# Four row buffers with y built in place, and the chunk stage's loads in written order, in a hybrid decoder step on Trainium2

## The chip, the cores and the metric

The kernel runs on one core of a Trainium2 chip. Its engines are PE (TensorE, matmuls, with PEld for the weight loads), DVE (VectorE), ACT (ScalarE), POOL (GpSimd) and SP (SyncE), which here does nothing but issue DMA transfers. Each engine works through its own list of instructions in order, and semaphores order them against each other. The metric is device microseconds of one execution, and a kernel's time is the median of several runs.

## The reference, cut to what matters

One layer of a decoder with two branches, for 1024 prompt positions and 64 sample positions (8 samples of 8 positions each). Pooling branch `P` and state-space branch `S` share one input projection, and are merged by gates.

```python
proj = h @ w_in
u_pool, z_pool, z_ssm, xbc, dt_raw, g_raw = jnp.split(proj, SPLITS, axis=-1)
p, pool_new = pool_mix(u_pool, pool_buf, pos0, pool_w, pool_scale)
p = (p * jax.nn.silu(z_pool)) @ w_pool_out
xbc_c, conv_new = causal_conv(xbc, conv_buf, conv_w, conv_b)
...
y, ssm_new = ssd(xs, dt, A, Bm, Cm, ssm_state)
y = (y + d_skip.astype(jnp.float32)[:, None] * xs).reshape(b, L, D_INNER)
y = rmsnorm(y * jax.nn.silu(z_ssm.astype(jnp.float32)), ssm_norm_g)
s = y.astype(x.dtype) @ w_ssm_out
gates = jax.nn.sigmoid(g_raw)
m = gates[..., :D_MODEL] * p + gates[..., D_MODEL:] * s
x = x + gate[:, None] * (m @ w_o)
```

`ssd` goes over the prompt in 8 chunks of 128 positions, for 4 groups of 8 heads, and carries a state from chunk to chunk:

```python
def step(h, inp):
    xq, dq, Bq, Cq = inp
    acs = jnp.cumsum(dq * Ag, axis=1)
    seg = acs[:, :, None] - acs[:, None, :]
    decay = jnp.exp(jnp.where(mask, seg, -jnp.inf))
    cb = jnp.einsum('bign,bjgn->bijg', Cq, Bq)
    att = cb[..., None] * decay * dq[:, None]
    y = jnp.einsum('bijge,bjgep->bigep', att, xq)
    y = y + jnp.einsum('bign,bige,bgepn->bigep', Cq, jnp.exp(acs), h)
    ...
```

## The kernel before, in words

The kernel goes in stages: the norm and the first gate products; the input projection (seven products in place of eight for each pair of column blocks) with the convolutions and the pooling beside it; the samples' state-space part beside the last of these; then the chunk stage; then a tail with the last group's output products, w_o and the final norm. Intermediate results lie in DRAM (`xbc_d`, `z_d`, `gp_d`, `ys_d` and others). A planner decides the order of the instructions on each engine from a simulated timeline, unless the text fixes it: `in_line(engines)` chains all instructions of the named engines that were written since the last call, so that they run in written order, and `behind(engine)` puts what is written under it behind that engine's latest instruction.

The chunk stage is the one that the change touches. It does two things side by side.

- 32 rows, one for each group g and chunk c: the generator `chunk(g, c)`, in steps divided by `yield`. Step 1 loads the row's x, B and C (`xb`, six blocks of 128 x 128, line 1491) and the decay exponents (`dec`, 512 KB, line 1187). Step 2 makes the exponentials: `cE` on ACT (1498), the mask `far` on POOL (1192), eight exponentials on ACT (1201). Step 3 loads silu(z) (`sz`, 1504), transposes x and B on PE (1507, 1509), and scales on DVE (1518, 1520, 1525, 1527). Step 4 does the row's products on PE (1532, 1213, 1216) and the state (1538, 1540), adds D times x into a tile `v` on DVE (1545), and calls `finish`. `finish` multiplies `v` by `sz` on DVE (1468), rounds it into the high half `yh` on ACT (1470), squares it on ACT (1471), subtracts for the low half `yl` on POOL (1472), and sums the squares on POOL (1473 to 1479). A fifth step, in the last chunk of a group alone, stores the state.
- 32 products of weights with a whole block of rows, from the generator `pieces`: 8 of the pooling branch (`P_unit`, which loads a gate row `sg` at 1718, multiplies it at 1721 and stores it), then 8 for each of the groups 0 to 2 (`S_unit`). Each is three PSUM blocks of 12 matmuls (359 to 361). The weights come from DRAM by `ready` (459 and 460) into tiles with four buffers. `products(t)` has made 2.56 blocks for each row by time t, beyond the first four.

From row 13 on, `wo_splits` adds the splitting of w_o into high and low halves, 16 pieces: load (1771), high half on ACT (1775) and its store, low half on POOL (1777) and its store by SP (1781). It has two buffers for the raw pieces, so a load waits for the store of the low half two pieces before.

`sample_end(g)` brings in the 64 sample positions of a group: it loads their silu(z) (1483) and their sums `ys` (1485) and calls `finish`, once in eight rows.

In turn i of the main loop (line 1802) come: a step of `wo_splits`, step 3 of row i+1, products up to i+0.4, a fifth step of row i-1 if there is one, a step of `wo_splits`, step 4 of row i, step 1 of row i+3, step 2 of row i+2, products up to i+1. PE runs in written order throughout, DVE and ACT only in the part before the loop, SP in the planner's order.

Buffers before: `xb` three, `dec` three, `cE` two, `sz` three, `v` two (shared by rows and samples), PSUM tiles `mm` three.

Of the kernel before, what the change touches and what calls it, by code (L numbers as in the profile page):

```python
# [11 lines left out]
ALU = mybir.AluOpType  # L12
# [8 lines left out]
P = 128  # L21
# [4 lines left out]
NS = 64  # L26
# [7 lines left out]
NC = SEQ // CH  # L34
# [12 lines left out]
def tile_pool_ssd_step(  # L47
# [9 lines left out]
    def nm(s):  # L57
        uid[0] += 1
        return f"{s}_{uid[0]}"
# [37 lines left out]
    def PB():  # L97
        return psB.tile([P, 512], F32, tag="ps", name=nm("ps"))
# [8 lines left out]
    def const(shape, name, dt=F32):  # L107
        return cp.tile(shape, dt, tag=name, name=name)
# [5 lines left out]
    V = nc.vector  # L114
# [224 lines left out]
    def in_line(engines, begin=False):  # L339
        traced = nc.cur_bb.bb.instructions  # L340
        for i in traced[len(traced) if begin else line[0]:]:
            if i.engine in engines:
                if i.engine in line[1]:
                    tc.add_manual_dep(i, line[1][i.engine], mybir.DependencyInfo(
                        mybir.DependencyClass.NoSync, mybir.DependencyReason.DATA), reason="in_line")
                line[1][i.engine] = i.name
        line[0] = len(traced)
# [20 lines left out]
    Dv = const([P, 16], "Dv")  # L368
# [815 lines left out]
    def decays(dec, g, c):  # L1184

        S = P if c < NC else NS
        load(dec, acs_d[c, 8 * g:8 * g + 8, :S].partition_broadcast(S))
# [275 lines left out]
    def ckt(shape, tag, bufs=2):  # L1463
        return (cl if tag in CKL else ca if tag in ("dec", "xb", "cE") else ck).tile(list(shape), F32, tag=tag, name=nm(tag), bufs=bufs)

    def finish(g, o, S, v, sz):

        V.tensor_tensor(v, v, sz, ALU.mult)
        yhc = yh[g][:, :, o:o + S]
        act(yhc, v, AF.Copy)  # L1470
        act(sz, v, AF.Square)
        nc.gpsimd.tensor_tensor(yl[g][:, :, o:o + S], v, yhc.bitcast(F32), ALU.subtract)
        nc.gpsimd.tensor_tensor(sz[:, 0:2], sz[:, 0:2], sz[:, 2:4], ALU.add)
        sa = sq_acc[:, o:o + S]
        if g == 0:
            nc.gpsimd.tensor_tensor(sa, sz[:, 0], sz[:, 1], ALU.add)
        else:
            nc.gpsimd.tensor_tensor(sz[:, 0], sz[:, 0], sz[:, 1], ALU.add)
            nc.gpsimd.tensor_tensor(sa, sa, sz[:, 0], ALU.add)

    def sample_end(g):
        sz = ckt([P, 4, P], "sz", 3)[:, :, :NS]
        load(sz, z_d[g][:, :, SEQ:])
        v = ckt([P, 4, P], "v")[:, :, :NS]
        load(v, ys_d[g])
        finish(g, SEQ, NS, v, sz)

    def chunk(g, c):
        o = c * P
        xb = ckt([P, 6, P], "xb", 3)  # L1490
        load(xb, xbc_d[g][:, :, o:o + P])
        Bf, Cf = xb[:, 4], xb[:, 5]
        dec = ckt([P, 8, P], "dec", 3)
        decays(dec, g, c)
        yield
        if c > 0:
            cE = ckt([P, 8, P], "cE")
            act(cE, dec, AF.Exp, scale=-1.0)
        if g > 0 or c > 0:
            far(dec, c)  # L1500
            exps(dec, g, c)
            yield
        sz = ckt([P, 4, P], "sz", 3)
        load(sz, z_d[g][:, :, o:o + P])
        px = PB()
        for q in range(4):
            nc.tensor.transpose(px[:, q * P:(q + 1) * P], xb[:, q], ident)
        pbc = PB()
        nc.tensor.transpose(pbc[:, :P], Bf, ident)
        mm(pbc[:, P:2 * P], Bf, Cf, start=True, stop=True)  # L1510
        bt = ckt([P, P], "bt", 2)
        act(bt, pbc[:, :P], AF.Copy)
        if c > 0:
            act(pbc[:, 2 * P:3 * P], Cf, AF.Copy)
        pxv = px.rearrange("p (h d) -> p h d", d=64)
        heads = slice(8 * g, 8 * g + 8)
        xd = ckt([P, 8, 64], "xd", 2)
        V.tensor_tensor(xd, pxv, dtT[:, c, heads].unsqueeze(2).to_broadcast([P, 8, 64]), ALU.mult)
        xw = ckt([P, 8, 64], "xw", 1)
        V.tensor_tensor(xw, pxv, wdT[:, c, heads].unsqueeze(2).to_broadcast([P, 8, 64]), ALU.mult)  # L1520
        if g == c == 0:
            yield
            far(dec, c)
            exps(dec, g, c)
        V.tensor_tensor(dec, dec, pbc[:, P:2 * P].unsqueeze(1).to_broadcast([P, 8, P]), ALU.mult)
        if c > 0:
            V.tensor_tensor(cE, cE, pbc[:, 2 * P:3 * P].unsqueeze(1).to_broadcast([P, 8, P]), ALU.mult)
        yield
        if c == 0:
            yh[g], yl[g] = [Y4(hs if g % 2 else hp) for _ in range(2)]  # L1530
        pu = PC()
        mm(pu, bt, xw.rearrange("p h d -> p (h d)"), start=True, stop=True)  # L1532
        pi = inner(xd, dec, P, *((hst[g], cE) if c > 0 else ()))
        hn = ckt([P, 512], "hst", 2)
        if c == 0:
            act(hn, pu, AF.Copy)
        else:
            nc.gpsimd.tensor_tensor(hn.rearrange("p (h d) -> p h d", d=64), hst[g].rearrange("p (h d) -> p h d", d=64),
                                    Elb[:, c, heads].unsqueeze(2).to_broadcast([P, 8, 64]), ALU.mult)
            V.tensor_tensor(hn, hn, pu, ALU.add)  # L1540
        hst[g] = hn

        v = ckt([P, 4, P], "v")
        for q in range(4):
            V.scalar_tensor_tensor(v[:, q], xb[:, q], Dv[:, 4 * g + q:4 * g + q + 1], pi[:, q], ALU.mult, ALU.add)
        finish(g, o, P, v, sz)
        if c == NC - 1:
            yield
            pt = PB()
            for q in range(4):  # L1550
                nc.tensor.transpose(pt[:, q * P:(q + 1) * P], hn[:, q * P:(q + 1) * P], ident)
            fo = ckt([P, 4, P], "fo", 1)
            act(fo, pt.rearrange("p (q n) -> p q n", n=P), AF.Copy)
            store_(new_ssm_p[0, 0, 8 * g:8 * g + 8].rearrange("(q h) p n -> (h p) q n", h=2), fo)
# [192 lines left out]
    prods = []  # L1747
# [7 lines left out]
    def pieces():  # L1755
        ws = first_ws
        nxt = len(ws)
        for i, (pf, run) in enumerate(prods):
            while nxt < len(prods) and nxt <= i + 1:
                ws[nxt] = prods[nxt][0]()  # L1760
                nxt += 1
            yield from run(ws.pop(i))
# [3 lines left out]
    def wo_splits():  # L1766
        raws = {}
        for n in range(18):
            if n < 16:
                raws[n] = ck.tile([P, 512], F32, tag="pw", name=nm("pw"), bufs=2)  # L1770
                load(raws[n], w_o[0, n // 2 * P:n // 2 * P + P, n % 2 * 512:n % 2 * 512 + 512])
            yield
            if 0 < n < 17:
                hi = ck.tile([P, 512], F32R, tag="ph", name=nm("ph"), bufs=1)
                act(hi, raws[n - 1], AF.Copy)
                store_(wo_d[(n - 1) // 2][:, 0, (n - 1) % 2 * 512:(n - 1) % 2 * 512 + 512], hi.bitcast(F32))
                nc.gpsimd.tensor_tensor(raws[n - 1].bitcast(F32R), raws[n - 1], hi.bitcast(F32), ALU.subtract)
                lo = raws.pop(n - 1)
            yield
            if 0 < n < 17:  # L1780
                load(wo_d[(n - 1) // 2][:, 1, (n - 1) % 2 * 512:(n - 1) % 2 * 512 + 512], lo)
    wos = wo_splits()
    RATE = 2.56
    FRONT = 4
# [5 lines left out]
            next(pc_, None)  # L1790
            made += 1

    first_engines = (mybir.EngineType.PE, mybir.EngineType.Activation, mybir.EngineType.DVE)
    in_line(first_engines, True)
    next(seq[0])
    for _ in range(FRONT - 1):
# [5 lines left out]
    for i in range(len(seq)):  # L1802
        if i > 12:
            with behind(mybir.EngineType.Activation), behind(mybir.EngineType.SP), behind(mybir.EngineType.Pool):
                next(wos, None)
        if i + 1 < len(seq):
            next(seq[i + 1])
        products(i + 0.4)
        if i > 0:
            next(seq[i - 1], None)  # L1810
        if i > 12:
            with behind(mybir.EngineType.Activation), behind(mybir.EngineType.SP), behind(mybir.EngineType.Pool):
                next(wos, None)
        next(seq[i], None)
        if i % NC == 3:
            sample_end(i // NC)
        if i + 3 < len(seq):
            next(seq[i + 3])
        if i + 2 < len(seq):
            next(seq[i + 2])  # L1820
        products(i + 1.0)
    next(seq[-1], None)
    for it in (pc_, wos):
        for _ in it:
            pass
    in_line((mybir.EngineType.PE,))
    right.__exit__(None, None, None)
    while right_all:
        right_all.pop().__exit__(None, None, None)
# [152 lines left out]
    for i in range(8):  # L1982
# [7 lines left out]
        if last_:  # L1990
            q, s3 = hs.tile([P, T], F32, tag="sq", name="q", bufs=1)[:, :D], const([P, 4], "s3")
# [61 lines left out]
```

## Time and profile before

| | us |
|---|---|
| median of 3 runs | 1296.55 |
| lowest, highest | 1295.5, 1297.77 |
| the profiled execution | 1301.79 |
| its span, from the first instruction to the last | 1300.1 |
| mean granted clock of PE in it | 0.992 |

The profile is of one execution on the chip. In its lists, a line such as `L1507` is a line of the kernel, `out<-in` names the tiles by the program's names, and `x4` counts instructions that were merged. `PE` is the matmul, `PEld` the weight load, `SPq` a DMA issue on SP. In a row in order of time the first number is the start, the second the duration, and the bracket at its end gives the idle time of the engine just before it and what ended it. A row of waits gives the total, how often, and the longest. Two parts of the page show where the span goes in 40 equal slices and over the chain of work that ended last:

```profile
PE   7999999999999999999999999989999999999998
...
DMA  9837345465455544444565566988768788574621
...
PE 62%; issue 7%; DMA 6%; POOL 4%; DVE 3%; ACT 2%; ACTq 0%; SPq 0%; POOLq 0%; DVEq 0%
```

A digit is the busy share of a slice of 32.5 us in tenths. The chunk stage is about slices 26 to 35, in which the 16 DMA engines are busier than in most of the rest.

### The profile page before, as it was taken

The page shows a single profiled execution, that of the slowest core. Times are in us where ns is not written, and L with a number is a line of the kernel's source. Part 1 is how long each engine was busy: PE and PEld are TensorE (multiplying, and loading weights), DVE is VectorE, ACT ScalarE, POOL GpSimd, SP SyncE. Part 2 cuts the span into 40 slices and gives each one's busy share as a digit, 9 for nine tenths or more (in the row PEclk, how much of TensorE's full clock was granted, in tenths as well). Part 3 has the DMA queues.
Part 4 walks back from the last instruction along what each step waited for, and adds up shares of the span by engine and source line. Part 5 has one row for each costly group of instructions (what it writes and reads, how often), then busy time and mean ns, then how long its engine had stood idle before and what let it go on. Part 6 is the DMA issues. An engine that isn't in the chain of part 4 may idle for free.

```text
span 1300.1 us, 26323 instructions
## 1 busy us (share of the span) xinstructions
PE 1263.0 (97%) x9739; PEld 1173.4 (90%) x9739; DVE 901.5 (69%) x1608; ACT 662.4 (51%) x1528; POOL 668.3 (51%) x563
## 2 busy tenths in 40 slices
PE   7999999999999999999999999989999999999998
PEld 6779999989999999999999999978898888999786
DVE  4685778966979688776776765667676777476433
ACT  4665347364656655556556544555676655201111
POOL 1007669676869777565444435245566758214000
PEclk9999999999999999999999999999999999999999
DMA  9837345465455544444565566988768788574621
GB/s 330 253 108 226 115 148 175 145 207 162 139 170 198 174 154 135 155 144 134 169 193 173 174 183 200 343 263 264 248 212 281 243 286 262 177 260 160 227 104 51
DMA packets 233793, 251.68 MB, mean 194 GB/s; under 512 B 31265, under 2 KB 177905, under 8 KB 233658
## 3 DMA queue, kind: packets, MB, share of 16 engines
q1 hardware_dynamic: 161568, 171.60, 42.1%
q10 hardware_dynamic: 72098, 78.41, 17.8%
q8 instruction: 77, 1.26, 0.4%
q14 instruction: 50, 0.41, 0.1%
HBM read 167.06 MB, written 83.01 MB: 192 GB/s over the span
## 4 chain that ended last, share of the span: by engine, by line
PE 62%; issue 7%; DMA 6%; POOL 4%; DVE 3%; ACT 2%; ACTq 0%; SPq 0%; POOLq 0%; DVEq 0%
PE ps L608 6%; PE ps L609 6%; PE ps L610 6%; PE mm L608 6%; PE mm L610 6%; PE mm L609 5%; PE mm L359 4%; PE mm L360 3%; PE mm L361 3%; PE ps L1213 2%; PE ps L1999 2%; PE ps L2001 2%; PE ps L2000 2%; PE pc L1532 2%; POOL wlo L168 2%
## 5 line engine op out<-in xcount | busy, mean ns | idle before, releaser
L168 POOL TENSOR_TENSOR wlo<-rawA,whi 128x512 fp32r<-128x512 f32 x120 | 179.9, 1503 | 176.3 <-ACT whi L165 101.5
L168 POOL TENSOR_TENSOR wlo<-raw,whi 128x512 fp32r<-128x512 f32 x92 | 149.1, 1627 | 122.8 <-ACT whi L165 111.9
L359 PE MATMUL mm<-Y,whi 128*128 128x352 f32 (+1 forms) x480 | 165.7, 345 | 0.6 <-DVE G L1902 0.5
L360 PE MATMUL mm<-Y,whi 128*128 128x352 f32 (+1 forms) x480 | 159.4, 332 | 0.3 <-DVE Y L1569 0.3
L361 PE MATMUL mm<-Y,wlo 128*128 128x352 f32 (+1 forms) x480 | 158.7, 331 | 0.0
L608 PE MATMUL mm<-Y,whi 128*128 128x272 f32 x496 | 146.6, 296 | 0.7 <-DVE GA L624 0.5
L608 PE MATMUL ps<-Y,whi 128*128 128x272 f32 x496 | 144.2, 291 | 2.7 <-ACT o L808 2.1
L610 PE MATMUL mm<-Y,wlo 128*128 128x272 f32 x496 | 144.5, 292 | 2.2 <-POOL wlo L168 1.5
L609 PE MATMUL ps<-Y,whi 128*128 128x272 f32 x496 | 143.8, 290 | 0.0
L610 PE MATMUL ps<-Y,wlo 128*128 128x272 f32 x496 | 143.4, 289 | 0.0
L609 PE MATMUL mm<-Y,whi 128*128 128x272 f32 x496 | 142.9, 288 | 0.0
L1056 DVE SCALAR_TENSOR_TENSOR GA<-GA,cvT,GA 128x1112 f32<-128x1112 f32 x72 | 129.6, 1803 | 0.8 <-ACT GA L1053 0.7
L165 ACT ACTIVATE whi<-rawA 128x512 fp32r<-128x512 f32 x125 | 78.3, 627 | 91.4 <-PE ps L609 47.3
L165 ACT ACTIVATE whi<-raw 128x512 fp32r<-128x512 f32 x96 | 58.9, 627 | 105.2 <-DVE raw L554 48.0
L359 PEld LDWEIGHTS mm<-Y,whi 128*128 128x128 f32 x480 | 91.9, 191 | 7.1 <-issue 4.8
L610 PEld LDWEIGHTS mm<-Y,wlo 128*128 128x128 f32 x496 | 93.6, 189 | 4.0 <-POOL wlo L168 2.4
L608 PEld LDWEIGHTS ps<-Y,whi 128*128 128x128 f32 x496 | 94.0, 190 | 3.3 <-ACT o L808 2.3
L608 PEld LDWEIGHTS mm<-Y,whi 128*128 128x128 f32 x496 | 93.4, 188 | 3.3 <-ACT whi L165 0.7
L1201 ACT ACTIVATE dec<-dec,acT 128x128 f32<-128x128 f32 (+1 forms) x288 | 86.5, 383 | 18.4 <-POOL dec L1192 18.0
L609 PEld LDWEIGHTS mm<-Y,whi 128*128 128x128 f32 x496 | 93.7, 189 | 0.9
L609 PEld LDWEIGHTS ps<-Y,whi 128*128 128x128 f32 x496 | 94.1, 190 | 0.0
L610 PEld LDWEIGHTS ps<-Y,wlo 128*128 128x128 f32 x496 | 94.1, 190 | 0.0
(448 smaller groups left out, 3764.3 us busy)
## 6 DMA issues: line engine op xcount, KB each, us to landing
rawA<-in_w_in SPq DMA_DIRECT2D x46, 512.0 KB
dec<-acs_d SPq DMA_DIRECT2D x32, 512.0 KB
xbc<-GA ACTq DMA_DIRECT2D x24, 512.0 KB
xb<-xbc SPq DMA_DIRECT2D x32, 384.0 KB
rawA<-in_w_in SPq DMA_DIRECT2D x32, 256.0 KB
pw<-in_w_ssm_out ACTq DMA_DIRECT2D x32, 256.0 KB
ws<-ph ACTq DMA_DIRECT2D x32, 256.0 KB
ws<-pw SPq DMA_DIRECT2D x32, 256.0 KB
```

The lines of the kernel that those rows point to most:

```text
L165: ins = act(hi[:, :, :ncols], raw[:, :, :ncols], AF.Copy)
L168: (eng or nc.gpsimd).tensor_tensor(lo[:, :, :ncols], raw[:, :, :ncols], hi[:, :, :ncols].bitcast(F32), ALU.subtract)
L359: mm(ps[:, :n], a, rh[k][:, o:o + n], start=(k == 0), stop=False)
L360: mm(ps[:, :n], a, rl[k][:, o:o + n], start=False, stop=False)
L361: mm(ps[:, :n], b, rh[k][:, o:o + n], start=False, stop=(k == nk - 1))
L608: mm(p, hi, ah, start=(k == 0), stop=False)
L609: mm(p, hi, al, start=False, stop=False)
L610: mm(p, lo, ah, start=False, stop=(k == 3))
L1056: V.scalar_tensor_tensor(d[:, :n], rp[:, k:k + n], cvT[:, 24 * k + mc:24 * k + mc + 1], d[:, :n], ALU.mult, ALU.add)
L1201: act(dec[:, h], dec[:, h], AF.Exp, bias=acT[:S, c, 8 * g + h:8 * g + h + 1], scale=-1.0)
L1213: mm(o[hh], xd[:S, 2 * q + hh, :], dec[:S, 2 * q + hh], start=True, stop=state is None)
L1532: mm(pu, bt, xw.rearrange("p h d -> p (h d)"), start=True, stop=True)
```

## The change

Five edits, all in the chunk stage:

- `v` is no tile of its own for a row but the first four blocks of the row's `xb`; the multiply-add 1545 works in place, and so does `finish`. `xb` has four buffers. The samples' `v` is a tile of its own with one buffer, now contiguous.
- `sample_end` becomes a generator: it loads at the row with i % 8 = 2 and finishes at the row with i % 8 = 4; before, both were at i % 8 = 3.
- `pieces` asks for weights up to two products ahead, not one.
- `wo_splits` loads a raw piece and splits the piece before it in one step, and stores the low half in the next; before, the load came with the store of the low half before it, and the split in the step between.
- SP joins the engines whose instructions are chained in written order, in the part before the loop and in the loop.

```diff
     def sample_end(g):
         sz = ckt([P, 4, P], "sz", 3)[:, :, :NS]
         load(sz, z_d[g][:, :, SEQ:])
-        v = ckt([P, 4, P], "v")[:, :, :NS]
+        v = ckt([P, 4, NS], "v", 1)
         load(v, ys_d[g])
+        yield
         finish(g, SEQ, NS, v, sz)
 
     def chunk(g, c):
         o = c * P
-        xb = ckt([P, 6, P], "xb", 3)
+        xb = ckt([P, 6, P], "xb", 4)
...
-        v = ckt([P, 4, P], "v")
+        v = xb[:, 0:4]
         for q in range(4):
-            V.scalar_tensor_tensor(v[:, q], xb[:, q], Dv[:, 4 * g + q:4 * g + q + 1], pi[:, q], ALU.mult, ALU.add)
+            V.scalar_tensor_tensor(v[:, q], v[:, q], Dv[:, 4 * g + q:4 * g + q + 1], pi[:, q], ALU.mult, ALU.add)
         finish(g, o, P, v, sz)
...
-            while nxt < len(prods) and nxt <= i + 1:
+            while nxt < len(prods) and nxt <= i + 2:
                 ws[nxt] = prods[nxt][0]()
...
                 raws[n] = ck.tile([P, 512], F32, tag="pw", name=nm("pw"), bufs=2)
                 load(raws[n], w_o[0, n // 2 * P:n // 2 * P + P, n % 2 * 512:n % 2 * 512 + 512])
-            yield
             if 0 < n < 17:
                 hi = ck.tile([P, 512], F32R, tag="ph", name=nm("ph"), bufs=1)
...
             yield
             if 0 < n < 17:
                 load(wo_d[(n - 1) // 2][:, 1, (n - 1) % 2 * 512:(n - 1) % 2 * 512 + 512], lo)
+            yield
...
-    first_engines = (mybir.EngineType.PE, mybir.EngineType.Activation, mybir.EngineType.DVE)
+    first_engines = (mybir.EngineType.PE, mybir.EngineType.Activation, mybir.EngineType.DVE, mybir.EngineType.SP)
...
-        if i % NC == 3:
-            sample_end(i // NC)
+        if i % NC == 2:
+            ends = sample_end(i // NC)
+            next(ends)
+        if i % NC == 4:
+            next(ends, None)
...
-    in_line((mybir.EngineType.PE,))
+    in_line((mybir.EngineType.PE, mybir.EngineType.SP))
```

## The prediction

> **What bounds the kernel now.** I read the page first, then the busy times by stretch, the waits, the engines' rows in order of time, and SP's own waits.
>
> ```profile
> span 1300.1 us, 26323 instructions
> PE 1263.0 (97%) x9739; PEld 1173.4 (90%) x9739; DVE 901.5 (69%) x1608; ACT 662.4 (51%) x1528; POOL 668.3 (51%) x563
> ```
>
> PE is busy for 97% of the span, and the change touches only the chunk stage, about 817 to 1140 us. So the question is how much PE time that stage loses. The columns below are PE, PEld, DVE, ACT and POOL busy, then the granted clock, the DMA share and GB/s.
>
> ```profile
> core 0: us, PE busy (x) PEld busy (x) DVE busy (x) ACT busy (x) POOL busy (x), PEclk, DMA share, GB/s
> 817.00:866.00 49.00, 48.40 (x358) 43.42 (x357) 36.49 (x61) 28.91 (x75) 18.68 (x20) 1.00 0.93 308
> 866.00:881.00 15.00, 10.96 (x68) 8.74 (x66) 7.63 (x14) 5.80 (x16) 5.62 (x8) 0.77 0.82 264
> 881.00:1024.00 143.00, 143.00 (x1164) 127.36 (x1164) 102.32 (x176) 89.80 (x233) 88.80 (x105) 1.00 0.79 251
> 1024.00:1049.00 25.00, 22.16 (x172) 19.50 (x171) 19.55 (x36) 16.89 (x46) 14.89 (x17) 1.00 0.87 271
> 1049.00:1094.00 45.00, 44.89 (x355) 39.72 (x354) 31.74 (x55) 27.28 (x67) 33.06 (x38) 1.00 0.87 266
> 1094.00:1108.00 14.00, 12.12 (x90) 10.17 (x90) 12.03 (x24) 8.64 (x25) 9.77 (x14) 0.88 0.80 244
> ...
> 876.50:880.50 4.00, 4.00 (x15) 3.85 (x15) 3.36 (x9) 3.35 (x11) 1.69 (x2) 0.55 0.90 282
> ...
> 1102.50:1106.50 4.00, 4.00 (x16) 3.81 (x16) 3.94 (x9) 2.03 (x7) 2.25 (x3) 0.64 0.87 272
> ```
>
> The loss sits in three places: 4.04 us idle from 866 to 881, 2.84 from 1024 to 1049, 1.88 from 1094 to 1108. Behind the first and the last the clock is down: 0.55 of four microseconds (1.80 us lost) and 0.64 of four (1.44 us). Elsewhere PE is full, 143.00 of 143. What PE waited for, from its rows in order of time:
>
> ```profile
> 873.18 1.02 PE L1507 MATMUL ps<-ident,xb 128*128 128x128 f32 x4 [2.24 <-DMA xb<-xbc]
> 876.00 0.45 PE L1509 MATMUL ps<-ident,xb 128*128 128x128 f32 x1 [1.81 <-DVE cE L1527]
> ...
> 1036.69 0.55 PE L1507 MATMUL ps<-ident,xb 128*128 128x128 f32 x3 [1.33 <-DMA xb<-xbc]
> ...
> 1047.64 0.63 PE L1507 MATMUL ps<-ident,xb 128*128 128x128 f32 x4 [1.08 <-DMA xb<-xbc]
> ...
> 1101.65 0.80 PE L1507 MATMUL ps<-ident,xb 128*128 128x128 f32 x4 [1.88 <-DMA xb<-xbc]
> ```
>
> Four of the five are the transposes of a row (L1507) waiting for its `xb` to land, 6.53 us. The fifth, 1.81, is a PSUM buffer that DVE freed late. DVE was late for a reason of its own, in its waits and rows:
>
> ```profile
> DVE v L1468 <- DMA v<-ys: 17.2, 4, 7.4
> ...
> 872.05 0.43 DVE L1468 TENSOR_TENSOR v<-v,sz 128x256 f32<-128x256 f32 x1 [7.42 <-DMA v<-ys]
> ...
> 1089.89 0.83 DVE L1468 TENSOR_TENSOR v<-v,sz 128x256 f32<-128x256 f32 x1 [3.50 <-DMA v<-ys]
> ```
>
> Four times, once a group, DVE stands before the samples' sums `ys`, which are loaded and used in the same turn. The two waits quoted precede the first and the last loss; the other two, 6.3 us together, precede none.
>
> **The change, part by part.**
>
> *Row buffer and y in place.* The four multiply-adds L1545 and everything in `finish` keep engine, shape and count, so no work is added or removed; only `v` lies in the row's own `xb`. Three `xb` buffers become four. Today the load for row r+3 waits for row r's L1545; the chain of waits shows it:
>
> ```profile
> 1034.25 1.25 POOL Y L1472
> ...
> 1039.57 1.11 DVE v L1545 x4
> 1040.68 0.03 DVE G L1742
> 1040.71 6.79 DMA xb<-xbc
> ...
> 1095.71 5.80 DMA xb<-xbc
> ```
>
> L1545 ends at 1040.68, the load goes at 1040.71, lands 6.79 us later, and PE had waited 1.08 us. After the change that load waits for the previous row's last reader, POOL's subtraction L1472, which ended at 1035.50: 5.2 us earlier, against the 1.08 needed. The largest of the four waits is 2.24. So all four, 6.53 us, should go where POOL is as prompt as here.
>
> *Samples' sums two rows ahead.* The loads move from the turn in which they are used to two turns before it. The pace of a row:
>
> ```profile
> L1532 PE MATMUL pc<-xw,bt x64: 590/592/596, 831.2 to 1115.4; 128*128 128x512 f32 x64
> ...
> SPq L1771 <- DMA wo<-pw: 50.5, 14, 5.4
> SPq L459 <- PE mm L361: 35.0, 13, 9.0
> SPq L1504 <- POOL sq_acc L1479: 19.0, 12, 2.6
> SPq L1718 <- DMA m<-R: 18.9, 5, 6.3
> ```
>
> 31 row steps from 831.2 to 1115.4 are 9.2 us each, so the sums get some 18 us; the longest wait is 7.42. DVE's 17.2 us go, and with them PE's 1.81. One `v` buffer of its own suffices: it is used once in eight rows. The `sz` rotation is as before, one extra allocation in eight.
>
> *Clock.* If the gaps go, the 1.80 and 1.44 us go too: 3.24. The Trainium skill's page "TensorE: Matmul & The Clock Gate", section "HAM oscillation — how this bites in real kernels", has it that idle gaps above about 3.4 us drop the clock. By that rule the 1.88 us gap would cost nothing further and the sum would be smaller by 1.44; the 0.64 behind that gap says otherwise, so the row decides.
>
> *SP in written order.* The last rows above are SP's own waits. The longest, 50.5 us, is the raw w_o load (L1771) waiting for the store of the low half whose buffer it takes; the moved `yield` puts half a row between the two, so this falls mostly away. What a wait blocks is everything written behind it. Per row that is: w_o load, `sz` of the next row, weights and gate rows, low-half store, `xb` and `dec` three rows on. The pace is set by `dec`, which waits for row r's products, so SP comes by once a row; each `xb`, `sz` and weight load has more than one row of lead, 9.2 us, against 5.8 to 6.8 to land. I cost this at nothing; it hides behind the products on PE. The ends for the range: no gain, and the 16.2 us of the slower rival.
>
> *Weights two products ahead.* Today's order already issues them as soon as one of the four buffers is free (35.0 us of waits for L361 are these), thus three or more products ahead. Written order makes that two. A product is three PSUM blocks, and 2.56 blocks go with a row, so 10.8 us each: 21 us of lead. Nothing gained, nothing lost.
>
> *Gate rows of the pooling products.* These, L1718, are the one load that comes later. Products 1 to 7 now load their `R` in the order in which the product starts; today they run ahead (and wait, 18.9 us, for older stores).
>
> ```profile
> 819.18 0.42 SPq L1718 DMA_DIRECT2D R<-gp  x1
> ...
> 827.28 0.55 DVE L1721 TENSOR_TENSOR R<-mm,R 128x384 f32<-128x384 f32 x1
> ...
> 1025.06 0.17 PE mm L359
> ```
>
> From issue to use 8.1 us lie here, an upper bound of what the load needs. A product's first block is 12 matmuls at 0.17 us, 2.0 us, so DVE may stand up to 6.1 us at L1721, seven times. The bounds: DVE waits of some 3.1 us (the two without loss) cost PE nothing, so the lower end is 0; 3.50 and 7.42 us came with gaps of 1.88 and 4.04, so at 6.1 perhaps 3, seven times 21 us. The wait is nearer the lower end, since `mm` has three PSUM buffers and the block that needs the same one starts 10.8 us later: I take 2.0.
>
> **Sum.** 6.53 + 1.81 + 3.24 = 11.58 gained, 2.0 given back: 9.6 us. The profiled execution goes from a span of 1300.1 (1301.79 with what lies around it) to 1290.5. The runs shown have a median of 1296.55, 5.2 below that execution; less 9.6 this is **1287.0**. Its own range: down to 1282.2, if the remaining idle time goes too (0.42 in the three places, 0.60 and 0.11 in their neighbours) and the clock loss of 866 to 881 is the whole 0.23 × 15 = 3.45 instead of 1.80; up to 1291 with 6 us given back instead of 2.0.
>
> **Rivals.**
>
> *Gate rows late.* Three or four of the seven DVE waits cost PE about 2 us each: 7.5 given back, 1292.5. For it: 0.93 DMA share from 817 to 866, where most of these loads fall. Against it: DVE is idle for 12.5 of those 49 us.
>
> *It does not do what it says.* The row's load is freed earlier but leaves no earlier, since the written order puts it behind `sz` (19.0 us of waits for POOL) and the low-half store; the gaps stay or move: 1296.5. For it: right after a samples' turn the `sz` buffer asked for was released only one row ago. Against it: a late `sz` in front of `xb` is one wait of some ten microseconds in eight rows.
>
> *Slower: the row's reload now hangs on POOL.* L1472 must end the landing time before the transposes four rows on. In one stretch of today's run it doesn't; POOL stands behind a mask that waits for ACT:
>
> ```profile
> POOL dec L1192 <- ACT cE L1498: 29.3, 6, 14.3
> ...
> 1048.81 1.30 POOL L1472 TENSOR_TENSOR Y<-v,Y 128x512 fp32r<-128x512 f32 x1 [1.83 <-ACT Y L1470]
> ...
> 1071.88 2.56 POOL L1472 TENSOR_TENSOR Y<-v,Y 128x512 fp32r<-128x512 f32 x2 [1.47 <-ACT Y L1470]
> ...
> 1054.97 0.60 PE L1507 MATMUL ps<-ident,xb 128*128 128x128 f32 x4
> ...
> 1074.36 0.60 PE L1507 MATMUL ps<-ident,xb 128*128 128x128 f32 x4
> ```
>
> By count these are rows 22 and 24 (ends 1050.11 and about 1073.16) and the transposes of 26 and 28, 4.86 and 1.20 us later. With 5.8 to 6.8 to land, PE would stand 0.9 to 1.9 and 4.6 to 5.6 us, plus about 1.6 of clock: 8.1 at the middle for a group. In one group the change still wins 3.5; from two groups on it loses, 16.2 − 11.6 = 4.6, and with the 2.0 above 6.6: 1303. Against it: the low-half store and the mask's `dec` load, which made POOL late there, stood behind the 50.5 us. The Trainium skill's page "DMA: Bandwidth & Descriptors", section "Anatomy of one DMA", says that a DMA's semaphore wait is spent on the issuing sequencer before dispatch; SP's rows agree, and this is why a late POOL would hold the weights and `dec` as well, and why I don't go lower with this case.
>
> **How the numbers follow.** Forecast 0.55, gate rows late 0.15, no effect 0.12, slower 0.18. 0.2% (2.6 us) is about what a measurement of this kernel tells from none; the three runs lie within 2.3 us. Faster is the first two, 0.70; same 0.12; slower 0.18. The range 1282 to 1299 holds the first three, and leaves out most of the fourth.
>
> **What would show it.** Right: no PE wait for `xb` above 0.5 us and none of DVE for `ys`; granted clock 1.00 from 866 to 881 and 1094 to 1108; SP's wait L1771 far under 50.5. The 2.0 would be DVE's wait at L1721 for the gate rows, absent today. Wrong: PE waits for `xb` whose load left right after L1472 (the slower case); DVE waits for gate rows with PE gaps before 900 us (the first rival); or gaps of the same size at other rows.

## The result, and the profile after

| | before | changed |
|---|---|---|
| median, us | 1298.66 | 1305.33 |
| lowest, highest, us | 1295.5, 1308.41 | 1299.13, 1310.13 |
| the profiled execution, us | 1301.79 | 1308.79 |
| its mean granted clock | 0.992 | 0.99 |

Both medians are of 18 runs. The ratio is 1.0047, with a 95% interval of 1.003 to 1.0064: the change makes the kernel slower by about 6 us, where 1287.0 was forecast in a range that ends at 1299. Line numbers of the changed kernel are one higher than before's from the loads of `chunk` on, up to the w_o load (the lines behind it, 1775 to 1781, are as before): the transposes are L1508 and L1510, the loads of `xb` and `sz` L1492 and L1505, the multiply-add L1546, the gate row's load and multiply L1719 and L1722, the w_o load L1772.

The page of the changed kernel:

```profile
span 1307.1 us, 26274 instructions
PE 1263.8 (97%) x9739; PEld 1174.2 (90%) x9739; DVE 899.7 (69%) x1608; ACT 662.5 (51%) x1528; POOL 669.5 (51%) x563
...
PE 58%; issue 8%; DMA 8%; POOL 6%; DVE 4%; ACT 2%; SPq 0%; ACTq 0%; POOLq 0%; DVEq 0%
```

Busy times are those of before within 2 us. The work is the same. Of the 7.0 us between the spans of the two profiled executions PE's busy time takes 0.8; in the other 6.2 PE stood. In the chain that ended last, DMA has gone from 6% to 8% and POOL from 4% to 6%.

The busy times by stretch, with the columns as before (PE, PEld, DVE, ACT, POOL, clock, DMA share, GB/s):

```profile
864.00:880.00 16.00, 11.20 (x70) 9.35 (x69) 9.87 (x19) 4.98 (x13) 5.51 (x7) 0.79 0.82 271
...
1018.00:1024.00 6.00, 3.16 (x28) 2.70 (x25) 4.01 (x8) 0.95 (x3) 3.75 (x5) 1.00 0.83 236
1024.00:1057.00 33.00, 33.00 (x266) 29.17 (x266) 22.48 (x39) 20.48 (x52) 20.33 (x22) 1.00 0.91 305
1057.00:1080.00 23.00, 20.17 (x158) 17.76 (x157) 17.74 (x29) 12.58 (x33) 15.37 (x19) 1.00 0.60 199
1080.00:1092.00 12.00, 9.40 (x67) 8.21 (x66) 7.58 (x18) 6.24 (x16) 7.06 (x9) 0.86 0.90 295
1092.00:1110.00 18.00, 18.00 (x149) 16.04 (x148) 15.44 (x25) 11.95 (x29) 14.83 (x18) 1.00 0.92 296
```

The loss sits in four places now: 4.80 us idle from 864 to 880, 2.84 from 1018 to 1024, 2.83 from 1057 to 1080, 2.60 from 1080 to 1092; behind the first and the last the clock is down. The last of the three losses of before is gone: from 1092 to 1110 PE is busy for 18.00 of 18 us, at a clock of 1.00. What PE waited for, from its rows in order of time:

```profile
870.34 0.69 PE L359 MATMUL mm<-Y,whi 128*128 128x384 f32 x1 [4.80 <-DVE R L1722]
...
1023.86 0.63 PE L1508 MATMUL ps<-ident,xb 128*128 128x128 f32 x4 [2.84 <-DMA xb<-xbc]
...
1059.79 0.66 PE L1508 MATMUL ps<-ident,xb 128*128 128x128 f32 x4 [1.56 <-ACT fo L1554]
...
1061.72 0.33 PE L1510 MATMUL ps<-ident,xb 128*128 128x128 f32 x1 [1.27 <-DVE cE L1528]
...
1083.42 0.63 PE L1508 MATMUL ps<-ident,xb 128*128 128x128 f32 x4 [2.60 <-DMA xb<-xbc]
```

So a gate row, the `xb` of row 22, a PSUM buffer before row 26, and the `xb` of row 28 (rows are counted from 0, eight to a group). PE's 9739 matmuls stand in the same order in both traces, so the start of each after can be set against the start of the same one before. This sum over single rows, worked out beside the profile's views, gives the account. The left column is the time of before.

| stretch of before, us | later at its begin, at its end, us | so | what lies there |
|---|---|---|---|
| 0 to 817 | 0, 1.37 | +1.4 | the stages ahead, untouched |
| 817 to 868 | 1.37, 9.29 | +7.9 | new: the gate row, its clock |
| 868 to 884 | 9.29, 2.63 | −6.7 | gone: the gaps of 2.24 and 1.81, their clock |
| 884 to 1015 | 2.63, 3.54 | +0.9 | |
| 1015 to 1020 | 3.54, 6.56 | +3.0 | new: `xb` of row 22 |
| 1020 to 1050 | 6.56, 3.11 | −3.5 | gone: the gaps of 1.33 and 1.08 |
| 1050 to 1058 | 3.11, 6.30 | +3.2 | new: PSUM before row 26 |
| 1058 to 1080 | 6.30, 10.64 | +4.3 | new: `xb` of row 28, its clock |
| 1080 to 1110 | 10.64, 6.70 | −3.9 | gone: the gap of 1.88, its clock |
| 1110 to the end | 6.70, 7.01 | +0.3 | |

The five gaps of before are gone, and 14.1 us came from that. New ones took 18.4, and 2.6 are spread. Why the new ones arose stands in the waits. First DVE's for the gate rows, from 800 to 1150 us:

```profile
DVE R L1722 <- DMA R<-gp: 13.9, 6, 4.2
```

Then SP's own in the same stretch:

```profile
SPq L1781 <- POOL pw L1777: 38.8, 9, 6.0
SPq L1492 <- ACT sz L1471: 28.2, 8, 5.2
SPq L1492 <- POOL Y L1472: 21.4, 11, 12.9
...
SPq L1772 <- DMA wo<-pw: 17.3, 10, 4.3
SPq L1505 <- POOL sq_acc L1479: 13.6, 7, 8.1
SPq L1505 <- ACT sz L1471: 11.1, 3, 5.7
```

DVE's wait for `ys` has gone from 17.2 to 0.9, and SP's wait for the store of the low half has gone from 50.5 to 17.3. But now SP stands for the low half's subtraction (38.8), for the readers of the row buffer (28.2 and 21.4) and for free `sz` buffers (13.6 and 11.1), each time at the head of its list. SP's issues in order of time show what stood behind it, in three places: before the gate row, before row 22's `xb`, and before row 28's.

```profile
860.81 0.52 SPq L1505 DMA_DIRECT2D sz<-z  x1
...
862.51 0.43 SPq L1719 DMA_DIRECT2D R<-gp  x1
...
1016.27 0.52 SPq L1505 DMA_DIRECT2D sz<-z  x1
...
1017.56 0.52 SPq L1492 DMA_DIRECT2D xb<-xbc  x1
...
1066.21 0.39 SPq L1781 DMA_DIRECT2D wo<-pw  x1
1079.61 0.53 SPq L1492 DMA_DIRECT2D xb<-xbc  x1
```

An `sz` load keeps SP from 853.0, the end of the issue before it, to 860.81, and three issues on, at 862.51, goes the gate row, 4.5 us after PE had ended the block that it is for (858.0 by PE's rows). It lands at 869.7, when DVE has stood for it 3.71 us and PE for DVE's PSUM buffer nearly 4.80. An `sz` load after the samples' turn keeps it from 1006.2 to 1016.27, and at 1017.56 goes row 22's `xb`, 6.3 us before PE takes it: 3.5 us before PE was free for it, and 2.84 in which PE stood. The load of row 28's `xb` itself keeps it from 1066.6 to 1079.61. What that one waited for stands in the chain of waits:

```profile
1078.30 1.30 POOL Y L1472
1079.61 3.67 DMA xb<-xbc
```

This is row 24's subtraction. It ends at 1079.60, the load leaves at 1079.61, lands 3.67 us later, and PE stands. DVE had finished row 24's product with `sz` at 1065.6: from there to POOL's end it is 14.0 us.

The fourth place, before row 26, has a longer chain. SP had stood from 1037.6 to 1043.60 for the low half of a w_o piece, and row 25's `dec` left behind that store:

```profile
1043.60 0.32 SPq L1781 DMA_DIRECT2D wo<-pw  x1
...
1044.64 0.64 SPq L1187 DMA_DIRECT2D dec<-acs_d  x1
```

ACT waited 4.14 us for it, until 1050.85, and was late from there on with the copies that row 26's PSUM buffers hang on. That the rest of the delay follows from this wait is read from the order of ACT's rows and was not tested.

### The profile page after: what moved, and what is told of

Its sections match the earlier page's. It is cut to its first block, busy times and chain, and to the rows that moved or that the text cites. A ratio compares the mean times of both kernels' runs of the same rounds, so it can differ in the third digit from the quotient of the medians.

```text
span 1307.1 us, 26274 instructions
## 1 busy us (share of the span) xinstructions
PE 1263.8 (97%) x9739; PEld 1174.2 (90%) x9739; DVE 899.7 (69%) x1608; ACT 662.5 (51%) x1528; POOL 669.5 (51%) x563
## 4 chain that ended last, share of the span: by engine, by line
PE 58%; issue 8%; DMA 8%; POOL 6%; DVE 4%; ACT 2%; SPq 0%; ACTq 0%; POOLq 0%; DVEq 0%
PE ps L608 6%; PE ps L609 6%; PE ps L610 6%; PE mm L608 6%; PE mm L610 6%; PE mm L609 5%; PE mm L359 3%; PE mm L360 3%; PE mm L361 3%; PE ps L2004 2%; PE ps L2003 2%; PE ps L2005 2%; PE ps L1213 2%; POOL G L1912 2%; DMA dec<-acs_d 1%
```

## The experiments

Three theories stood for the new gaps. **Written order**: SP's list is now in written order, so a wait for an `sz` buffer or a gate row asked for too late holds up what is due sooner. **In place**: the row buffer hangs on POOL, as the prediction's slower rival had it. **By chance**: the gaps are accidents of one execution. Each experiment ran in five rounds beside the kernel before; the ratios are to that, with 95% intervals. "PE waits" names the waits of PE above 1 us from 810 to 1150 us in the profiled execution.

### e1_planner: the change without the written order

```diff
-    first_engines = (mybir.EngineType.PE, mybir.EngineType.Activation, mybir.EngineType.DVE, mybir.EngineType.SP)
+    first_engines = (mybir.EngineType.PE, mybir.EngineType.Activation, mybir.EngineType.DVE)
...
-    in_line((mybir.EngineType.PE, mybir.EngineType.SP))
+    in_line((mybir.EngineType.PE,))
```

> The changed kernel with SP back in the planner's order; the four buffers, y in place, the samples' sums and the w_o steps stay. If the written order of SP is the whole loss (one late load holds all behind it), the forecast's gain of about 11 us comes out: some 1287 where before is 1298.7. If y in place is the loss, since the row's buffer hangs on the low half's subtraction, the planner's order moves the other loads past it but the late row stays: about 1300, and PE still waits near 1080 us for xb. Gate rows go early again, so no PE gap before 900 us in either case.

1293.68 us against 1298.01, 0.9966 (0.9957 to 0.9976). PE waits: 2.21 before row 26 and 3.53 for row 28's `xb`, no others. The gate row and row 22 cost nothing here; the places of rows 26 and 28 stay. So the first two gaps come from the written order; the last two arise without it as well. The two ratios, 1.0047 and 0.9966, though not from the same rounds, are about 10.5 us apart, close to the 7.9 and 3.0 that the account gives to the first two places.

### e2_own_sz: the samples' silu(z) in a tile of its own

```diff
-        sz = ckt([P, 4, P], "sz", 3)[:, :, :NS]
+        sz = ckt([P, 4, NS], "zs", 1)
```

> The changed kernel with a tile of their own for the samples' silu(z), so that the rows' three sz buffers rotate undisturbed. If the sz load after a samples' turn is what holds SP (7.7 us before 1016.3 in the changed kernel's trace, then xb at 1017.6 for a transpose due at 1020.7), the gap of 3.0 us there goes, and the gate row behind the sz at 860.8 comes 7 us earlier, so the gap of 5 us at 865 shrinks too: 6 to 10 us less than the changed kernel. If SP is held by something else, no difference.

1297.69 against 1298.01, 0.9998 (0.9985 to 1.0011). The gap before row 22 is gone, and its `xb` leaves 9.4 us before PE is free for the transposes, not 3.5. The gate row's gap has become one of 2.75 for a later product's. 4.43 before row 26 and 1.03 for row 28 stay. That one runs through `dec`, as rows of this experiment show, from POOL, SP, ACT and DVE in turn:

```profile
1042.27 1.28 POOL L1472 TENSOR_TENSOR Y<-xb,Y 128x512 fp32r<-128x512 f32 x1
...
1043.58 0.53 SPq L1492 DMA_DIRECT2D xb<-xbc  x1
1044.20 0.58 SPq L1187 DMA_DIRECT2D dec<-acs_d  x1
...
1049.70 1.06 ACT L1499 ACTIVATE cE<-dec 128x1024 f32<-128x1024 f32 x1 [2.84 <-DMA dec<-acs_d]
...
1050.95 0.28 ACT L1515 ACTIVATE ps<-xb 128x128 f32<-128x128 f32 x1
...
1052.46 1.22 DVE L1528 TENSOR_TENSOR cE<-cE,ps 128x1024 f32<-128x1024 f32 x1
...
1053.93 1.09 PE L1508 MATMUL ps<-ident,xb 128*128 128x128 f32 x4 [4.43 <-DVE cE L1528]
```

Row 22's subtraction ends at 1043.55 and frees the buffer for row 26's `xb`, which leaves at once and lands in time. But row 26's `dec` is written behind it on SP. It lands when ACT has waited 2.84 us for it; row 25's copy is behind that on ACT, DVE's multiply behind the copy, and the PSUM buffer of row 26's transposes behind the multiply.

### e3_gate_ahead: gate rows asked for one product ahead

```diff
-            if m == 0:
-                sg = first_g[0]
-            else:
-                sg = R()
-                with behind(mybir.EngineType.SP):
-                    load(sg, gp_d[m])
+            sg = first_g[m]
+            if m < 7:
+                first_g.append(R())
+                load(first_g[m + 1], gp_d[m + 1])
```

> The changed kernel with each gate row loaded one product earlier. If DVE's wait for the gate row makes the gap at 865 us (5.0 us and the low clock behind it), that gap goes and 6 to 8 us with it, about back to the kernel before; DVE's waits for gate rows (13.9 us) go to under 3. If the gap comes from the sz wait in front of it alone, the row is still held at that place and the gap stays.

1296.03 against 1298.01, 0.9986 (0.9975 to 0.9997). The gate row's gap is gone and nothing comes in its place there. PE waits: 3.26 for row 22's `xb`, 2.85 for row 28's.

### e4_first_row_v: a `v` of its own for a group's first row

```diff
-        v = xb[:, 0:4]
+        v = ckt([P, 4, P], "vr", 1) if c == 0 else xb[:, 0:4]
...
-            V.scalar_tensor_tensor(v[:, q], v[:, q], Dv[:, 4 * g + q:4 * g + q + 1], pi[:, q], ALU.mult, ALU.add)
+            V.scalar_tensor_tensor(v[:, q], xb[:, q], Dv[:, 4 * g + q:4 * g + q + 1], pi[:, q], ALU.mult, ALU.add)
```

> The changed kernel, but the first row of each group builds y in a tile of its own (one buffer more), as all rows did before. Theory: the first row of the last group can't write its high half until PE has ended the products of the group two before, whose Y tile it takes, and in place this holds the row's xb and SP for 12.9 us, until 1079.6. Then the gap of 2.8 us at 1080 us and the low clock behind it go: 4 to 5 us less than the changed kernel. Rival, POOL being late in general (mask behind ACT): other rows hold xb as well and the gap stays or moves.

1297.51 against 1298.01, 0.9993 (0.9981 to 1.0006). PE waits: 1.84 for the gate row and 3.07 for row 22; rows 26 and 28 show none above 1 us (0.75 is left before row 26). Row 28's `xb` on SP and row 24's subtraction on POOL:

```profile
1056.82 0.53 SPq L1492 DMA_DIRECT2D xb<-xbc  x1
...
1068.77 1.30 POOL L1472 TENSOR_TENSOR Y<-vr,Y 128x512 fp32r<-128x512 f32 x1
```

The subtraction is as late as ever, and the load leaves 13 us ahead of its end. That is the gap of row 28 taken apart: POOL's lateness was there before the change too (the prediction's rows have it at 1071.88), and only the tie between the two makes it cost something. That the gap before row 26 shrank as well was not foreseen; row 22 still works in place there, and e3, which doesn't touch rows 22 to 26, has no more than 0.86 at that place either.

### e10_sz_gate and e5_three: two edits together, and with the products' pace

e10 has the edits of e2 and e3 together. e5 has these and a third: after the first eight rows the products go at 2.85 blocks a row, not 2.56.

```diff
-        while made < RATE * t:
+        while made < (RATE * t if t <= 8 else 8 * RATE + 2.85 * (t - 8)):
```

The reason for the third: row 24 is the first of the last group. `finish` writes its high half into a tile that the output products of group 1 still read, and there are two such tiles. Those products are 8 of the pooling branch, 8 of group 0 and 8 of group 1, or 72 blocks. At the end of row 24's turn 4 + 2.56 × 25 = 68 have been made. At the faster pace it is 4 + 2.56 × 8 + 2.85 × 17 = 72.9.

> The changed kernel with the samples' own silu(z) tile and the gate rows one product earlier, 2.56 blocks a row as before. The gaps near 865 and 1020 go, the ones near 1055 and 1080 stay: by the third theory 5 to 9 us more than with the rate changed as well, a ratio near 0.996. If the two mends alone give 0.989, the group's first row cost nothing.

> The changed kernel with all three places mended, SP still in written order: a tile of their own for the samples' silu(z), each gate row one product earlier, and 2.85 blocks a row instead of 2.56 from row 8 on, so that PE has ended the products of the group two before when the last group's first row writes its high half. If the three waits are the whole of what the written order costs, the forecast's gain of 11 to 12 us comes out: a ratio to before of about 0.991. If the written order has a cost of its own beside them, it stays above the 0.9966 of the planner's order.

e10: 1293.23 against 1298.29, 0.9967 (0.9957 to 0.9977). PE waits: 3.78 before row 26, 1.04 for row 28's `xb` and 1.04 for the next; nothing before these. e5: 1285.51 against 1298.34, 0.9891 (0.986 to 0.9922), and no PE wait above 1 us in the whole stage. The stage in one stretch, of the changed kernel and then of e5:

```profile
817.00:1150.00 333.00, 318.31 (x2453) 284.58 (x2452) 225.14 (x398) 182.06 (x470) 181.85 (x210) 0.98 0.76 250
```

```profile
817.00:1150.00 333.00, 331.90 (x2565) 299.87 (x2564) 238.69 (x422) 183.56 (x472) 185.93 (x212) 0.99 0.81 267
```

PE stands 1.1 us in place of 14.7. Row 24 in e5, DVE's product, POOL's subtraction and the load behind it:

```profile
1057.61 1.07 DVE L1468 TENSOR_TENSOR xb<-xb,sz 128x512 f32<-128x512 f32 x1
...
1059.55 1.29 POOL L1472 TENSOR_TENSOR Y<-xb,Y 128x512 fp32r<-128x512 f32 x1
...
1060.87 0.53 SPq L1492 DMA_DIRECT2D xb<-xbc  x1
```

From the one's end to the other's end it is 2.2 us now, not 14.0: the products of group 1 were what held row 24. PE's rows agree: in the changed kernel the last matmul of group 1 (the 864th of the products, 24 of 36 each) ends at 1073.9 and ACT's copy of row 24 into the high half comes at 1077.03, while in e5 that matmul ends at 1050.6, ahead of DVE's product. SP's waits in e5:

```profile
SPq L1779 <- POOL pw L1775: 50.8, 14, 7.4
SPq L1492 <- ACT sz L1471: 39.1, 13, 6.0
...
SPq L1492 <- POOL Y L1472: 20.6, 21, 1.9
```

These three add up to 111 us, the same three of the changed kernel to 88. How long SP waits does not tell the kernel's time. What counts is whether anything that is due soon stands behind it.

### e11_before_rate and e12_planner_rate: the pace without the rest

e11 is the kernel before with the new pace alone. e12 is the change with the planner's order (e1) and the new pace.

> The kernel before with 2.85 blocks a row from row 8 on and nothing else. If the faster rate is worth much by itself, the three mends prove less: a ratio under 0.995. By the theory it frees the Y tile in time, which there holds no row buffer and no load: 0.998 to 1.002.

> The changed kernel with SP in the planner's order and the faster rate from row 8 on. The gaps that were left there near 1046 and 1069 us go (4 to 6 us): a ratio near 0.992, level with the three mends in written order. If written order is worth something in itself once the three are mended, this stays above 0.993.

e11: 1297.04 against 1298.29, 0.9992 (0.9978 to 1.0007): the pace by itself is worth nothing that can be told. e12: 1289.23 against 1298.29, 0.9946 (0.9929 to 0.9964). Its one PE wait above 1 us is 4.62 before row 26; row 28's gap is gone with row 24's lateness. The intervals of e12 and e5 do not overlap. But e5 also has the `sz` tile of its own and the gate rows asked for earlier; the planner's order with these two edits was not run, so that the written order itself is the better one is not shown.

e11 keeps the gaps of before at row 6 (1.38 and 2.29), has one of 1.58 for row 3's `xb`, and one of 2.51 before row 26, where DVE's multiply is late. In e11 `v` is a tile of its own, as before the change.

### e6_order_only, e7_inplace_only, e8_sums_only: one edit alone on the kernel before

e6 adds SP to the two `in_line` calls, and nothing else. e7 has four `xb`, `v` in place, and the samples' `v` in a tile of its own. e8 splits `sample_end` in two turns, with a `v` of its own.

> The kernel before with SP in written order and nothing else changed. Samples' loads and their use stay in one turn, w_o load right behind the store whose buffer it takes, three xb buffers. If the written order is the one harmful edit, this is slower than the changed kernel (over 1.005), with gate-row waits on DVE and the 50 us of waits for the w_o stores in front of xb. If it is harmless without y in place, about 1.000.

> The kernel before with y in place and four xb buffers alone, planner's order, samples as before. If the earlier release of the row buffer is worth what the forecast put down for it, the gaps at 1036, 1047 and 1101 us go (4 to 6 us) and the one at 873 stays in part, since DVE still waits for the sums: a ratio of 0.995 to 0.998. If the coupling to the low half costs as much as it brings, 1.000 or more, with xb waiting for L1472 of row 24.

> The kernel before with the samples' loads two rows ahead alone. DVE's 17 us of waits for ys go. Forecast: the 1.8 us and the low clock behind the first gap go, and part of the last gap, 3 to 5 us, a ratio of 0.996 to 0.998. Rival, the waits were cover for xb landing late anyway: about 1.000.

| | median, us | before, us | ratio | interval |
|---|---|---|---|---|
| e6_order_only | 1333.06 | 1298.34 | 1.0258 | 1.0221 to 1.0296 |
| e7_inplace_only | 1311.52 | 1298.34 | 1.0095 | 1.0066 to 1.0125 |
| e8_sums_only | 1295.27 | 1298.34 | 0.9973 | 0.9953 to 0.9993 |

e6, its waits from 800 to 1150 us, PE's and then SP's:

```profile
PE mm L359 <- DMA whi<-ws: 24.4, 8, 7.4
PE mm L359 <- DVE R L1721: 9.0, 3, 5.1
...
SPq L1771 <- DMA wo<-pw: 89.1, 14, 8.7
SPq L1491 <- DVE v L1545: 79.0, 19, 11.8
```

With weights asked for one product ahead, w_o's old steps and three `xb`, written order lets PE stand 24.4 us for weights and 9.0 us for PSUM blocks that DVE frees late at the gate rows, and SP 168 us at the two waits that those last two edits of the change shorten. Which of the missing edits does most was not separated; without any of them (the samples' loads are in one turn here too) the order costs 2.6%. In e7 SP still goes by the planner, but the tie to POOL acts at the same two places: PE waits 5.28 before row 26, 3.10 for row 28's `xb`, and 4.91 for row 24's and 3.30 at 839 beside. Without the edit to `wo_splits` SP's wait for the low half's store is 52.1 us, as before. So in place alone loses 12 us, and together with the edits of `wo_splits`, the samples and the weights (e1) it gains 4. Which of them makes the difference was not separated.

e8 gains about what was expected of it, and keeps PE waits of 1.19 and 2.42 for the `xb` of rows 3 and 6. It also has one before row 26, though `v` is not in place here and SP goes by the planner. ACT waits for row 26's `dec`, and DVE's multiply and PE's transposes follow, as in e2:

```profile
1047.82 1.06 ACT L1499 ACTIVATE cE<-dec 128x1024 f32<-128x1024 f32 x1 [2.17 <-DMA dec<-acs_d]
...
1052.06 0.63 PE L1508 MATMUL ps<-ident,xb 128*128 128x128 f32 x4 [1.63 <-DVE cE L1528]
```

So a late `dec` there needs neither the written order nor the row buffer's tie to POOL; before the change row 26's transposes began only 0.66 us after DVE's multiply had ended.

### e9_again: the changed kernel once more

> The changed kernel itself once more, on the chip of the next three. It should stand at 1.0047 of before within its interval, and its trace should show the gaps of the first one again: at the gate row near 865, at xb near 1020 and near 1080 us. If the gaps move from execution to execution, the three places were accidents of one trace.

1304.33 against 1298.29, 1.0057 (1.0037 to 1.0077). PE waits: 3.45 for the gate row, 2.94 for row 22's `xb`, 1.27 before row 26, 2.72 for row 28's `xb`. Every gap is back at its place, but for the first half of the one before row 26 (1.56 in the first execution, 0.23 here), so for the other three chance is out.

## Why the prediction was wrong

**The gaps of before** went, as forecast, and for the most part with the sizes given. For the first place 2.24, 1.81 and 1.80 had been put down, 5.85; 6.7 came. The 1.80 was taken over four microseconds, while the clock of before stands at 0.51 from 873.2 to 880.1, which is 3.4. For rows 24 and 25 it was 2.41 against 3.5, for the last place 3.32 against 3.9. All in all 11.58 were forecast and 14.1 came. Most of DVE's wait for `ys` and of SP's for the low half's store went too, as said.

**The step that failed** is "SP in written order", with its "I cost this at nothing; it hides behind the products on PE". The prediction had listed what each wait blocks, but took the lead of an `xb` at one row of 9.2 us and left out that the issue itself slips. Row 22's load left 3.5 us before PE was free for its transposes, since SP had stood 10 us for an `sz` buffer. The second rival had that very wait in its hands, "a late `sz` in front of `xb` is one wait of some ten microseconds in eight rows", and used it as an argument against itself. It was one wait of ten microseconds and cost 3.0 us. With the gate row (next paragraph) the written order cost 10.9 us, where nothing and 2.0 had been put down.

**Gate rows**: "I take 2.0" became about 8. The load was priced from its issue to its use, with the issue at the start of the product. In the run the issue came 4.5 us after that block's end, because SP stood at `sz`. Of DVE's six waits of 13.9 us together five cost PE no gap above 1 us, near what was argued (behind the longest, 4.23, PE stands 0.78 for DVE's next multiply); one cost a gap of 4.80, and at a clock of 0.79 for 16 us another 3.4. The experiments bear out both: e3 alone removes this gap, e2 alone moves it.

**The slower rival** was right about row 28. It named row 24 as late and put 4.6 to 5.6 us, and some clock, on the transposes of row 28; the account has 4.3, and e4 shows the mechanism. The case came in one group only, and for that the prediction says the change still wins. That is what e1 shows: with SP left to the planner the kernel is 4 us faster than before in spite of both gaps. The argument against the rival, that POOL was late only by what stood behind the 50.5 us, was false for row 24: this row waits for the products of group 1, whatever SP does. For row 26 the rival had the place, with 0.9 to 1.9 us against 3.2 in the account, but its reason is not shown for the changed kernel. The `xb` was in time and a `dec` was late, there behind the low half's store; in e2, e10 and e7 the `dec` goes right behind an `xb` that had waited for POOL's subtraction; and e8 and e11 have a gap there without `v` in place.

**Weights two products ahead**, "nothing gained, nothing lost": the lead was computed at 21 us and falls as low as 12.6 (issue at 1018.93, first matmul at 1031.5), which is still enough: PE doesn't wait for weights in the changed kernel; but in e6, with one product of lead under written order, it does, for 24.4 us.

**The sum**, then: 14.1 gained; 7.9, 3.0 and 7.5 lost; 2.6 spread over stretches that the change doesn't touch or that have no gap to name; net 6.9 slower, with rounding, against 7.0 between the two profiled executions and 6.7 between the medians. The chance of 0.70 for faster had no case in which two losses from the order came together with one group of the slower rival. The lower end of the range, 1282.2, needs more than the prediction says: with the idle and clock terms that it names the sum comes to 1284.2, and 1282.2 only if the 2.0 for gate rows falls away too. That e5's 1285.51 lies near the forecast is no support for it, since e5 has three edits that the prediction did not have.

**What stays open.** What makes the gap before row 26. In the changed kernel it is divided (1.56 for an ACT copy, 1.27 for DVE), and different loads kept `dec` back in different runs; why it is small in e3, e4 and e5 (0.86, 0.75 and 0.62) was not settled. So the 3.2 us there can't be given to one edit. A `v` of its own for all rows, with the rest of the change, was not tried.

## What to carry to other kernels

When loads are put in written order on one queue, go through the list once for each wait that can stand at its head, and count how late what is written behind it becomes; a load that is asked for where it is first needed (the gate rows) becomes late by the whole of that wait. Before a result is built in place in a load buffer, find the last reader's longest lateness, not its usual one: the reload inherits it, here 14 us once in 32 rows. When a large expected gain is missing, set the starts of the same instructions in both traces against each other: the gain was there, and so was the loss.

## What the runs showed of the hardware

The clock did not go by the length of the gap alone. Behind the gap of 4.80 us four microseconds stood at 0.50, and behind one of 2.60 four at 0.57, while behind one of 2.84 the clock stayed at 1.00:

```profile
870.00:874.00 4.00, 3.67 (x11) 3.67 (x12) 3.59 (x7) 1.32 (x3) 1.95 (x2) 0.50 1.04 389
...
1084.00:1088.00 4.00, 4.00 (x17) 3.88 (x16) 0.80 (x2) 1.57 (x4) 2.61 (x3) 0.57 0.98 301
```

Taken between its changes, the clock was 0.51 from 869.2 to 876.1 us and 0.51 from 1084.2 to 1087.7: 3.4 and 1.7 us lost. In the changed kernel 1024 to 1057 us, right behind the 2.84, shows 1.00. In e9 the same place has a gap of 2.94, and 0.62 from 1018 to 1022; in e4 it has one of 3.07, and 0.60 from 1016 to 1020. What decides between these was not tested. The Trainium skill, page "TensorE: Matmul & The Clock Gate", section "HAM oscillation — how this bites in real kernels", gives gaps above about 3.4 us as those to avoid; the 2.60 here, and the 1.88 before, lost clock below that figure.

The spread of single runs was larger than the first three told: these lay within 2.3 us, while 18 runs of the same kernel go from 1295.5 to 1308.41.
